# A bidirectional encoder block on one core: output projection begun where the input projection ends, modulation sums tied to tiles

## Chip, cores and metric

One core of a Trainium2 chip. The metric is the device time of one execution, in microseconds; lower is better.

## The reference

One layer on 1024 tokens of width 1024, in float32. A conditioning vector gives six modulation vectors; the input is normalised and modulated, projected once to the q, k, v of two kinds of attention, both are run, and one output projection with a gate is added to the residual. A gated feed-forward part (SwiGLU, width 2816) follows.

```python
mod = silu(c) @ w_ada + b_ada                  # six vectors: shift, scale, gate, twice
h = rms_norm(x, g_mix) * (1.0 + sc_m) + sh_m
proj = h @ w_in                                # 1024 x 3072: qa, ka, va, qb, kb, vb
o_a = neighbourhood_attention(qa, ka, va, rpb) # 8 heads of 64, window 8 x 16 on a 16 x 64 grid
o_b = differential_attention(qb, kb, vb, lam)  # 4 heads, two softmax maps each
o_b = rms_norm(o_b, subln_w) * (1 - lambda_init)
x = x + gt_m * (concatenate([o_a, o_b]) @ w_out)
h = rms_norm(x, g_ffn) * (1.0 + sc_f) + sh_f
gate, up = split(h @ w_gate_up)
x = x + gt_f * ((silu(gate) * up) @ w_down)
return rms_norm(x, g_final)
```

## The kernel before

Every large matmul is made of three, of high and low parts (high x high, high x low, low x high): a weight chunk or an activation tile is *split* into a high part, made by ScalarE (ACT), and a low part, the difference, made by VectorE (DVE) or GpSimd (POOL). For weights this is `split_into` (L201 ACT, L202 the low part, on POOL through most of attention).

The work of attention is a list of 64 *units* (`seq`): four pairs of heads of the neighbourhood attention (class `Na`), eight tiles of 128 queries each, then four heads of the differential attention (class `Da`), eight tiles each. A unit has these steps: `score` (PE's s or ns matmuls; DVE adds the bias and takes the minimum, L682 or L784, the min pass; ACT's exponential), `trans` (DVE scales, PE transposes at or nt, ACT copies the high part, DVE subtracts the low part: the unit's two *lows*, L705 or L814), `pv` (PE, for every second unit), and for `Da` `norm` and `finish` (ms, rda, bc: the norm of a head's output, which is stored to DRAM as `o_dram`).

Between these steps the main loop calls `fill(us)`, which takes matmuls off a queue of generators: the input projection's next q, k and v (`gen_qk`, `gen_v`), and at the end the first half of the output projection (`gen_mo`, matmul tiles mo, over the four pairs of the first kind of attention). `FILL` sets the amounts for each of the eight positions (pairs 0 to 3, heads 4 to 7). The second half of the output projection (tiles mpb and mp) follows when attention is done, then the feed-forward part (gu, dn).

Weights of the input projection come in 24 chunks of 512 KB: `load_next` splits the chunk that has come in and issues the load of the next, `next_w` takes a chunk. The modulation vectors that attention doesn't need are summed beside it by `gen_mods`: 48 loads wm of 256 KB, issued on POOL's queue (L587) into three buffers, and for each one step on DVE into `acc` (L596 the first of eight, L600 the others). The main loop takes one step to a unit (`next(mods, None)`). For the last unit of position 6, when the queue is empty, `load_late` loads the attention output (eight loads `ol`, L882), splits it (L888 ACT, L889 DVE), and loads, multiplies by the gate (L896) and splits the first chunks of w_out.

The program's order on each engine is not the order of the code: the scheduler that builds the program places each instruction by its own estimates, within the dependencies; `PE.after(a, b)` adds such a dependency without a semaphore, so that a stands behind b. Each engine then takes its instructions in that order.

## Time and profile before

| | us |
|---|---|
| runs (3) | 1422.79, 1429.08, 1430.99 |
| median | 1429.08 |
| the profiled execution, its own time | 1423.15 |
| its span, from the first to the last instruction | 1421.4 |

The profile holds one execution. An engine's busy time counts its own instructions; issuing a DMA or waiting for a semaphore is not busy. Matmuls are pipelined and their ends are modelled, so they overlap in the timeline. The granted clock is the share of TensorE's full clock in a stretch. The chain of waits is followed back from the last instruction, at each step to what released it. Times in the timeline count from the start of the span.

### The profile page before, as it was taken

The page shows a single profiled execution, that of the slowest core. Times are in us where ns is not written, and L with a number is a line of the kernel's source. Part 1 is how long each engine was busy: PE and PEld are TensorE (multiplying, and loading weights), DVE is VectorE, ACT ScalarE, POOL GpSimd, SP SyncE. Part 2 cuts the span into 40 slices and gives each one's busy share as a digit, 9 for nine tenths or more (in the row PEclk, how much of TensorE's full clock was granted, in tenths as well). Part 3 has the DMA queues.
Part 4 walks back from the last instruction along what each step waited for, and adds up shares of the span by engine and source line. Part 5 has one row for each costly group of instructions (what it writes and reads, how often), then busy time and mean ns, then how long its engine had stood idle before and what let it go on. Part 6 is the DMA issues. An engine that isn't in the chain of part 4 may idle for free.

```text
span 1421.4 us, 17696 instructions
## 1 busy us (share of the span) xinstructions
PE 1378.5 (97%) x7033; PEld 1142.2 (80%) x7033; DVE 724.2 (51%) x1324; ACT 461.9 (32%) x817; POOL 291.5 (21%) x318
## 2 busy tenths in 40 slices
PE   5899998999999999999999999999999999999997
PEld 5698787887898777787888888888888888888886
DVE  5775766748777589656747215113411421151136
ACT  5544444545445365423531220221121012202212
POOL 3021322311112000001430320421221132204201
PEclk8999999999999998999999999999999999999999
DMA  9231514433021251023321210211111121102102
GB/s 371 105 119 49 189 61 129 134 101 114 24 89 60 82 199 53 8 68 112 119 76 43 75 59 1 89 45 45 31 73 45 31 62 57 55 6 89 45 22 96
DMA packets 43826, 114.82 MB, mean 81 GB/s; under 512 B 12723, under 2 KB 12979, under 8 KB 42464
## 3 DMA queue, kind: packets, MB, share of 16 engines
q1 hardware_dynamic: 39280, 99.37, 20.8%
q0 software_dynamic: 4464, 14.33, 3.1%
q8 instruction: 55, 0.90, 0.3%
q14 instruction: 27, 0.22, 0.0%
HBM read 99.26 MB, written 14.42 MB: 80 GB/s over the span
## 4 chain that ended last, share of the span: by engine, by line
PE 90%; DVE 4%; ACT 2%; DMA 1%; issue 1%; POOL 1%; POOLq 0%; DVEq 0%; ACTq 0%
PE gu L89 33%; PE dn L89 17%; PE s L89 5%; PE pv L89 3%; PE mo L89 3%; PE k L89 3%; PE q L89 3%; PE mp L89 3%; PE at L89 2%; PE nk L89 2%; PE npv L89 2%; PE v1p L89 2%; PE v2p L89 2%; PE nq L89 1%; PE v3p L89 1%
## 5 line engine op out<-in xcount | busy, mean ns | idle before, releaser
L1126 DVE TENSOR_TENSOR sg<-sg,gu 128x512 f32<-128x512 f32 x44 | 30.2, 687 | 352.0 <-ACT sg L1125 352.0
L89 PE MATMUL dn<-wd_h,al 128*128 128x512 f32 x352 | 136.9, 389 | 0.0
L89 PE MATMUL dn<-wd_l,ah 128*128 128x512 f32 x352 | 136.9, 389 | 0.0
L89 PE MATMUL dn<-wd_h,ah 128*128 128x512 f32 x352 | 136.9, 389 | 0.0
L1156 DVE TENSOR_TENSOR dt<-dn,gate_f 128x512 f32<-128x512 f32 x96 | 66.4, 691 | 88.1 <-PE dn L89 88.1
L202 POOL TENSOR_TENSOR wg_l<-wg_r,wg_h 128x1024 fp32r<-128x1024 f32 x20 | 48.4, 2420 | 271.9 <-ACT wg_h L201 271.9
L684 ACT ACTIVATE p<-p,st 128x1024 f32<-128x1024 f32 x64 | 73.5, 1148 | 61.7 <-DVE st L682 58.7
L201 ACT ACTIVATE wg_h<-wg_r 128x1024 fp32r<-128x1024 f32 x22 | 23.3, 1060 | 212.2 <-PE dn L89 154.2
L89 PE MATMUL s<-qk 64*128 64x512 f32 x384 | 88.6, 425 | 2.9 <-DVE st L682 2.9
L682 DVE CUSTOM_DVE_ANT_0 p<-s,dist 128x1024 f32<-128x1024 f32 x64 | 77.1, 1218 | 23.7 <-PE s L89 22.8
L202 POOL TENSOR_TENSOR wd_l<-wd_r,wd_h 128x1024 fp32r<-128x1024 f32 x20 | 48.0, 2400 | 163.7 <-ACT wd_h L201 163.7
L89 PEld LDWEIGHTS dn<-wd_h,ah 128*128 128x128 f32 x352 | 66.1, 188 | 13.8
L89 PEld LDWEIGHTS dn<-wd_h,al 128*128 128x128 f32 x352 | 66.1, 188 | 13.7
L89 PEld LDWEIGHTS dn<-wd_l,ah 128*128 128x128 f32 x352 | 66.1, 188 | 13.7
L89 PEld LDWEIGHTS s<-qk 64*128 64x128 f32 x384 | 54.3, 189 | 26.0 <-issue 9.0
L1157 DVE TENSOR_TENSOR x<-x,dt 128x512 f32<-128x512 f32 x96 | 70.0, 729 | 2.9
L1125 ACT ACTIVATE sg<-gu 128x512 f32<-128x512 f32 x44 | 26.0, 590 | 138.4 <-PE gu L89 136.6
L89 PE MATMUL gu<-h2h,wg_h 128*128 128x512 f32 x176 | 68.9, 392 | 0.4 <-DVE sg L1126 0.4
L89 PE MATMUL gu<-h2l,wg_h 128*128 128x512 f32 x176 | 68.7, 391 | 0.0
L89 PE MATMUL gu<-h2h,wu_h 128*128 128x512 f32 x176 | 68.6, 390 | 0.0
L89 PE MATMUL gu<-h2l,wu_h 128*128 128x512 f32 x176 | 68.6, 390 | 0.0
L89 PE MATMUL gu<-h2h,wg_l 128*128 128x512 f32 x176 | 68.5, 389 | 0.0
(308 smaller groups left out, 3467.3 us busy)
## 6 DMA issues: line engine op xcount, KB each, us to landing
w_r<-in_w_in_dram SPq DMA_DIRECT2D x24, 512.0 KB, 3.7
wm<-in_w_ada_l_dram POOLq DMA_DIRECT2D x48, 256.0 KB, 3.5
wg_r<-in_w_gate_up_dram SPq DMA_DIRECT2D x22, 512.0 KB, 3.6
wu_r<-in_w_gate_up_dram SPq DMA_DIRECT2D x22, 512.0 KB, 3.5
wd_r<-in_w_down_dram SPq DMA_DIRECT2D x22, 512.0 KB, 3.5
x<-in_x_dram SPq DMA_DIRECT2D x16, 512.0 KB, 8.5
wada<-in_w_ada_s_dram SPq DMA_DIRECT2D x6, 1024.0 KB, 11.8
v<-vd SPq DMA_DIRECT2D x4, 1024.0 KB, 5.7
```

The costliest lines, as they stand in the source:

```text
L89: ins = call(*args, **kw)
L201: A.activation(out=hi, in_=raw, func=AF.Copy)
L202: lo_engine().tensor_tensor(out=lo, in0=raw, in1=hi.bitcast(F32), op=ALU.subtract)
L682: V.tensor_tensor_reduce(out=pr, in0=s, in1=dists[0][:, d0:d0 + 1024], scale=1.0, scalar=BIG, op0=ALU.add, op1=ALU.min, accum_out=self.st[ ...
L684: A.activation(out=pr, in_=pr, func=AF.Exp, scale=-1.0, bias=self.st[:, m:m + 1], accum_out=self.st[:, 2 + m:3 + m])
L1125: A.activation(out=sg, in_=gu[:, 0:512], func=AF.Silu)
L1126: V.tensor_tensor(out=sg, in0=sg, in1=gu[:, 512:1024], op=ALU.mult)
L1156: V.tensor_tensor(out=dt_, in0=out, in1=gtf[:, dsl], op=ALU.mult)
L1157: V.tensor_tensor(out=x1[i][:, dsl], in0=x1[i][:, dsl], in1=dt_, op=ALU.add)
```

## The change

Four things. (1) In `gen_qk` and `gen_v`, `load_next` stands behind the first half of a q or k, or the second of four tiles of a v, and no longer at the start. (2) `gen_mods` takes a function `mark`, and each of its steps on DVE is placed behind the instruction that `mark` names: in attention the last low that has been issued (`late_t["low"]`), in the feed-forward part the last addition of the output projection. Before, only the first step of each eight in the feed-forward part was tied. (3) `load_late` is called in the first unit of position 6 that finds the queue empty, behind that unit's `trans`; the first chunks of w_out are loaded and gated, and one is split, as soon as the last chunk of w_in has been taken (`pre_late`); o is loaded and split in two halves of four, and the second half and the chunks for the second 512 columns follow step by step, one to a unit (`late_steps`). (4) The fill of the last head is 29 for 36.

```diff
@@ -474,7 +474,6 @@
 
     def gen_qk(kind, key, name):
         w_h, w_l = next_w()
-        load_next()
         hd = key[1] + (4 if key[0][0] == "n" else 0)
         slot = qk_t(hd, 0 if kind == "q" else 2)
         mark = G.memset(slot[:, 0:1].bitcast(F32), 0.0)
@@ -491,11 +490,12 @@
                         mark = None
                 yield 0.65
             made = evac_q(out, hd, hf) if kind == "q" else evac_k(out, hd, hf)
+            if hf == 0:
+                load_next()
         qkv[key] = made
 
     def gen_v(n, evac):
         ws = [next_w(), next_w()]
-        load_next()
         for ip in range(4):
             out = bank(f"v{n}p{ip}")
             for ii in range(2):
@@ -511,6 +511,8 @@
                     if k % 2:
                         yield 0.65
             evac(n, ip, out)
+            if ip == 1:
+                load_next()
         qkv["vd", n] = True
 
     def v_tiles(n):
@@ -575,7 +577,9 @@
             tb.append(tbh)
         qkv["tb", pr] = tb
 
-    def gen_mods(steps, raw_of, acc_of, tmp_of, gate, queue, first=None, ahead=2):
+    late_t = {}
+
+    def gen_mods(steps, raw_of, acc_of, tmp_of, gate, queue, mark, ahead=2):
 
         steps = [(which, n, j) for which in steps for n in range(2) for j in range(KT)]
         raws = []
@@ -593,11 +597,11 @@
             yield
             if j == 0:
                 acc = acc_of(f"acc{which}{n}")
-                head = V.tensor_scalar(out=acc, in0=raws[at], scalar1=silc[:, 0:1], scalar2=None, op0=ALU.mult)
-                if first is not None:
-                    PE.after(head, first)
+                step = V.tensor_scalar(out=acc, in0=raws[at], scalar1=silc[:, 0:1], scalar2=None, op0=ALU.mult)
             else:
-                V.scalar_tensor_tensor(out=acc, in0=raws[at], scalar=silc[:, j:j + 1], in1=acc, op0=ALU.mult, op1=ALU.add)
+                step = V.scalar_tensor_tensor(out=acc, in0=raws[at], scalar=silc[:, j:j + 1], in1=acc, op0=ALU.mult, op1=ALU.add)
+            if mark() is not None:
+                PE.after(step, mark())
             if j < KT - 1:
                 continue
             if which in (3, 4):
@@ -702,7 +706,7 @@
                 src = tps.rearrange("p (a b) -> p a b", a=4)
                 hi, lo = at_h[b][:, :, e * P:(e + 1) * P], at_l[b][:, :, e * P:(e + 1) * P]
                 A.activation(out=hi, in_=src, func=AF.Copy)
-                V.tensor_tensor(out=lo, in0=src, in1=hi.bitcast(F32), op=ALU.subtract)
+                late_t["low"] = V.tensor_tensor(out=lo, in0=src, in1=hi.bitcast(F32), op=ALU.subtract)
 
         def pv(self, ats, pvs):
             h, i = self.h, self.i
@@ -811,7 +815,7 @@
                 src = tps[:, m * 512:m * 512 + nk].rearrange("p (a b) -> p a b", b=P)
                 dsl = (slice(None), slice(sl, sl + nk // P), slice(e * P, (e + 1) * P))
                 A.activation(out=pt_h[m][dsl], in_=src, func=AF.Copy)
-                V.tensor_tensor(out=pt_l[m][dsl], in0=src, in1=pt_h[m][dsl].bitcast(F32), op=ALU.subtract)
+                late_t["low"] = V.tensor_tensor(out=pt_l[m][dsl], in0=src, in1=pt_h[m][dsl].bitcast(F32), op=ALU.subtract)
 
         def pv(self, ats, pvs):
             pr, i = self.pr, self.i
@@ -870,9 +874,9 @@
         return gates[2]
 
     mods = gen_mods((2, 3, 4), mraw_t, lambda nm: mp.tile([P, 512], F32, tag="acc", bufs=1, name=nm),
-                    lambda nm, dt=F32: mp.tile([P, 512], dt, tag="sq", bufs=4, name=nm), gate_m, G)
-
-    oh, ol, wo, x1, late_t = [], [], [[], []], [], {}
+                    lambda nm, dt=F32: mp.tile([P, 512], dt, tag="sq", bufs=4, name=nm), gate_m, G, lambda: late_t.get("low"))
+
+    oh, ol, wo, x1 = [], [], [[], []], []
 
     o_at = {}
 
@@ -881,8 +885,8 @@
         for b in bs:
             SY.dma_start(out=o_at[n, b][1].bitcast(F32), in_=o_dram[n][:, b * 512:(b + 1) * 512])
 
-    def split_o(n, last=None):
-        for b in range(2):
+    def split_o(n, last=None, bs=(0, 1)):
+        for b in bs:
             dh, dl = o_at[n, b]
             full = last if b and last is not None else dl.bitcast(F32)
             A.activation(out=dh, in_=full, func=AF.Copy)
@@ -896,28 +900,57 @@
         V.tensor_tensor(out=both, in0=both, in1=gate, op=ALU.mult)
         wo[dh].append(split(raw, f"wo{dh}_{n2}"))
 
-    def load_late():
+    def gated(raw, dh):
+
+        both = raw.rearrange("p (a n) -> p a n", a=2)
+        gate = late_t["gtm"][:, dh * 512:(dh + 1) * 512].unsqueeze(1).to_broadcast([P, 2, 512])
+        V.tensor_tensor(out=both, in0=both, in1=gate, op=ALU.mult)
+        return raw
+
+    def pre_late():
+
         lo_eng[:] = [V]
         late_t["gtm"] = gates[2]
+        late_t["wo"] = [raw_t(f"wo0_{n2}r") for n2 in range(2)]
+        for n2, raw in enumerate(late_t["wo"]):
+            SY.dma_start(out=raw, in_=t["w_out"][0, n2])
+        for raw in late_t["wo"]:
+            gated(raw, 0)
+        wo[0].append(split_w(late_t["wo"][0], gp, "wo0_0"))
+
+    def load_late():
+
         for b in range(2):
             hi, lo = (gp.tile([P, 4, 512], F32R, tag="t8", bufs=8, name=f"o{z}{b}") for z in "hl")
             for n in range(4):
                 o_at[n, b] = hi[:, n, :], lo[:, n, :]
         for n in range(4):
-            load_o(n)
+            load_o(n, (0,))
         for n in range(4):
-            split_o(n)
-            if n % 2:
-                load_wo(0, n // 2, lambda raw, nm: split_w(raw, gp, nm))
-        ext = late_t["ext"] = qp_.tile([P, 4, S], F32R, tag="qk", name="ext")
-
-        def split(n2):
-            def f(raw, nm):
-                return split_into(raw, ext[:, 2 * n2, :], ext[:, 2 * n2 + 1, :])
-            return f
-
+            split_o(n, bs=(0,))
+            if n == 1:
+                wo[0].append(split_w(late_t["wo"][1], gp, "wo0_1"))
+        late_t["wo"] = []
         for n2 in range(2):
-            load_wo(1, n2, split(n2))
+            late_t["wo"].append(raw_t(f"wo1_{n2}r"))
+            SY.dma_start(out=late_t["wo"][-1], in_=t["w_out"][1, n2])
+            for n in (2 * n2, 2 * n2 + 1):
+                load_o(n, (1,))
+        late_t["steps"] = 0
+
+    def late_steps(upto):
+
+        while late_t["steps"] < upto:
+            i = late_t["steps"]
+            late_t["steps"] += 1
+            if i < 2:
+                for n in (2 * i, 2 * i + 1):
+                    split_o(n, bs=(1,))
+                continue
+            if i == 2:
+                late_t["ext"] = qp_.tile([P, 4, S], F32R, tag="qk", name="ext")
+            hi, lo = late_t["ext"][:, 2 * i - 4, :], late_t["ext"][:, 2 * i - 3, :]
+            wo[1].append(split_into(gated(late_t["wo"][i - 2], 1), hi, lo))
 
     def mo_part(out, dh, i, ns):
 
@@ -937,6 +970,7 @@
     def gen_mo(dh):
         dsl = slice(dh * 512, (dh + 1) * 512)
         for i in range(NT):
+            late_steps(4 if dh else 2 if i > 3 else 0)
             if dh == 0 and i % 2 == 0:
                 pair = gp.tile([P, 2, D], F32, tag="t8", bufs=8, name=f"x1_{i}")
                 for e in range(2):
@@ -946,7 +980,7 @@
             yield from mo_part(out, dh, i, range(4))
             V.tensor_tensor(out=x1[i][:, dsl], in0=out, in1=x1[i][:, dsl], op=ALU.add)
 
-    FILL = [34.0, 42.0, 24.0, 32.0, 23.0, 39.0, 34.0, 36.0]
+    FILL = [34.0, 42.0, 24.0, 32.0, 23.0, 39.0, 34.0, 29.0]
 
     SHARE = [(0.2, 0.3, 0.5), (0.25, 0.25, 0.5)]
 
@@ -981,6 +1015,8 @@
             for dh in range(2):
                 load_wo(dh, 2, lambda raw, nm: split_w(raw, gp, nm))
                 split_o(4 + dh)
+        if "steps" in late_t:
+            late_steps(min(late_t["steps"] + 1, 2 if u.pos < 7 else 4))
         share = SHARE[u.pos // 4]
         fill(step * share[0])
         if n >= 1:
@@ -993,14 +1029,16 @@
             seq[n - 3].finish()
         fill(step * share[1])
         next(mods, None)
-        if u.pos == 6 and u.i == 7:
+        if used[0] == len(PLAN) and "wo" not in late_t:
+            pre_late()
+        u.trans(ats)
+        if late_score:
+            nx.score()
+        if u.pos == 6 and "steps" not in late_t and (u.i == 7 or not queue):
             while queue:
                 fill(9)
             load_late()
             enqueue(7)
-        u.trans(ats)
-        if late_score:
-            nx.score()
         fill(step * share[2])
     for _ in mods:
         pass
@@ -1130,7 +1168,7 @@
             gtf = gate_t("gate_f")
             for _ in gen_mods((5,), lambda nm: lp.tile([P, 512], F32, tag="dt", bufs=4, name=nm),
                               lambda nm: lp.tile([P, 512], F32, tag="macc", bufs=1, name=nm),
-                              lambda nm, dt=F32: lp.tile([P, 512], dt, tag="sil", bufs=3, name=nm), lambda: gtf, SY, late_t["done"]):
+                              lambda nm, dt=F32: lp.tile([P, 512], dt, tag="sil", bufs=3, name=nm), lambda: gtf, SY, lambda: late_t["done"]):
                 pass
         wd = []
         for f in fs:
```

The order on DVE at the start of pair 1 (np, ptl: the unit's scaled exponentials and lows; acc: the modulation sums; vsl: a tile of v). Before:

```order
L803 TENSOR_SCALAR np_1_1465<-np_1_1465,nst_1_1464 128x384 x2
L814 TENSOR_TENSOR ptl_0_0_1541<-nt_0_1550,pth_0_0_1539 128x2x128
L600 SCALAR_TENSOR_TENSOR acc_1632<-wm_1410,silc,acc_1632 128x512
L814 TENSOR_TENSOR ptl_0_1_1542<-nt_0_1550,pth_0_1_1540 128x2x128
L616 TENSOR_TENSOR gate_m<-gt_1532,gb_1530 128x512
L600 SCALAR_TENSOR_TENSOR acc_1632<-wm_1537,silc,acc_1632 128x512
L600 SCALAR_TENSOR_TENSOR acc_1632<-wm_1634,silc,acc_1632 128x512
L784 ISA np_2_1591,nst_2_1590<-ns_2_1589,tb_1424 128x384
L784 ISA nst_2_1590 128x1
L784 ISA np_2_1591,nst_2_1590<-ns_2_1589,tb_1428 128x384
L784 ISA nst_2_1590 128x1
L600 SCALAR_TENSOR_TENSOR acc_1632<-wm_1709,silc,acc_1632 128x512
```

And now, from the same lows on:

```order
L818 TENSOR_TENSOR ptl_0_0_1541<-nt_0_1550,pth_0_0_1539 128x2x128
L818 TENSOR_TENSOR ptl_0_1_1542<-nt_0_1550,pth_0_1_1540 128x2x128
L600 TENSOR_SCALAR acc_1630<-wm_1340,silc 128x512
L620 TENSOR_TENSOR gate_m<-gt_1532,gb_1530 128x512
L788 ISA np_2_1591,nst_2_1590<-ns_2_1589,tb_1424 128x384
L788 ISA nst_2_1590 128x1
L788 ISA np_2_1591,nst_2_1590<-ns_2_1589,tb_1428 128x384
L788 ISA nst_2_1590 128x1
L788 ISA np_3_1662,nst_3_1661<-ns_3_1660,tb_1424 128x384
L788 ISA nst_3_1661 128x1
L540 TENSOR_TENSOR vsl_3_1609<-v3p_1512,vsh_3_1608 128x512
L788 ISA np_3_1662,nst_3_1661<-ns_3_1660,tb_1428 128x384
```

Of the four steps into acc that stood here one is left, behind the two lows of unit 0; the next stands further down, behind the lows of unit 1.

The order on PE where the output projection begins; in both, the last k matmul stands beside the transposes of unit 3 of position 6 (at_3) and the scores of its unit 5. Before (s_1: scores of unit 1 of the last head; at_7: transposes of the last unit of position 6):

```order
L89 MATMUL s_1_1_5414<-qk_4703 128x512 x6
L89 MATMUL at_7_0_5382<-ident,p_7_0_5244 128x128 x4
L89 MATMUL at_7_1_5389<-ident,p_7_0_5244 128x128 x4
L89 MATMUL mo_0_5399<-wo_0_h,oh_5326 128x512
L89 MATMUL mo_0_5399<-wo_0_h,ol_5327 128x512
```

And now (s_6: scores of unit 6 of position 6):

```order
L89 MATMUL mo_0_5217<-wo_1_h,oh_5186 128x512
L89 MATMUL mo_0_5217<-wo_1_h,ol_5187 128x512
L89 MATMUL mo_0_5217<-wo_1_l,oh_5186 128x512
L89 MATMUL s_6_1_5232<-qk_4353 128x512 x6
L89 MATMUL mo_1_5256<-wo_0_h,oh_5186 128x512
```

The first of the mo tiles has moved from behind the last unit of position 6 to ahead of the second half of the scores of its unit 6.

The order on PE at the end of attention, behind the last unit's transposes (at_7) and between its pv and its norm (ms). Before:

```order
L89 MATMUL at_7_0_6067<-ident,p_7_0_5940 128x128 x4
L89 MATMUL at_7_1_6074<-ident,p_7_0_5940 128x128 x4
L89 MATMUL mo_6_6082<-ext,oh_5328 128x512
L89 MATMUL mo_6_6082<-ext,ol_5329 128x512
L89 MATMUL mo_6_6082<-ext,oh_5328 128x512 x2
```

```order
L89 MATMUL mo_7_6124<-ext,oh_5328 128x512 x2
L89 MATMUL mo_7_6124<-ext,ol_5329 128x512
L89 MATMUL mo_7_6124<-ext,oh_5328 128x512
L89 MATMUL ms_1_6164<-mean_e,sq_1_6116 128x1 x4
L89 MATMUL bc_1_6179<-ident,rda_1_6169 128x128 x4
```

And now:

```order
L89 MATMUL mo_7_6079<-ext,oh_5188 128x512
L89 MATMUL at_7_0_6096<-ident,p_7_0_5982 128x128 x4
L89 MATMUL at_7_1_6103<-ident,p_7_0_5982 128x128 x4
L89 MATMUL pv_1_6018<-ath_3_0_6057,v_0_4828 128x256
L89 MATMUL pv_1_6018<-atl_3_0_6059,v_0_4828 128x256
```

```order
L89 MATMUL pv_1_6018<-ath_3_1_6058,v_0_4828 128x256
L89 MATMUL pv_1_6018<-atl_3_1_6060,v_0_4828 128x256
L89 MATMUL pv_1_6018<-ath_3_1_6058,v_1_4829 128x256
L89 MATMUL ms_1_6164<-mean_e,sq_1_6134 128x1 x4
L89 MATMUL bc_1_6179<-ident,rda_1_6169 128x128 x4
```

Twelve mo matmuls between at_7 and pv, and ten between pv and ms, have moved ahead of at_7; pv now follows the transposes and ms follows pv.

## Rows read from the trace of the kernel before

**Rows 1.** The page, parts 1 and 2: PE's busy time; its granted clock in 40 slices.

```profile
PE 1378.5 (97%) x7033; PEld 1142.2 (80%) x7033; DVE 724.2 (51%) x1324; ACT 461.9 (32%) x817; POOL 291.5 (21%) x318
...
PEclk8999999999999998999999999999999999999999
```

**Rows 2.** Windows: length, busy us of PE, PEld, DVE, ACT, POOL, clock, DMA, GB/s.

```profile
140.00:165.00 25.00, 22.68 (x160) 19.94 (x160) 22.42 (x51) 12.31 (x30) 8.48 (x13) 0.93 0.40 142
165.00:200.00 35.00, 35.00 (x190) 28.35 (x190) 22.35 (x60) 15.32 (x38) 10.01 (x23) 1.00 0.44 133
200.00:225.00 25.00, 20.11 (x114) 16.34 (x113) 20.05 (x46) 10.62 (x29) 7.84 (x18) 0.94 0.50 153
225.00:260.00 35.00, 34.48 (x241) 30.09 (x241) 21.65 (x63) 16.88 (x43) 7.41 (x24) 0.95 0.17 56
260.00:285.00 25.00, 23.57 (x177) 20.62 (x176) 20.55 (x55) 13.12 (x34) 11.65 (x24) 1.00 0.56 181
...
315.00:360.00 45.00, 42.45 (x195) 31.69 (x194) 33.54 (x63) 18.48 (x33) 8.78 (x10) 0.92 0.29 100
...
520.00:555.00 35.00, 34.51 (x165) 27.04 (x165) 33.83 (x61) 22.56 (x38) 1.01 (x1) 0.80 0.53 200
...
640.00:665.00 25.00, 23.40 (x104) 19.39 (x104) 15.52 (x23) 8.82 (x13) 1.09 (x2) 0.93 0.42 137
...
780.00:1421.00 641.00, 632.30 (x2790) 523.24 (x2788) 186.82 (x258) 115.19 (x165) 139.92 (x71) 1.00 0.16 51
```

**Rows 3.** The source line L600, the sums: ns min/median/max, first and last start.

```profile
L600 DVE SCALAR_TENSOR_TENSOR acc<-wm,silc,acc x56: 731/750/2964, 74.7 to 750.5; 128x512 f32<-128x512 f32 x56
```

**Rows 4.** The chain of waits from 155 to 281: start, us, what.

```profile
155.73 2.63 DVE acc L600
...
209.74 0.77 DVE acc L600
...
278.27 1.94 DVE acc L600
```

**Rows 5.** Timeline, sums on DVE and weight splits on POOL: start, us, instruction.

```profile
160.00 2.92 DVE L600 SCALAR_TENSOR_TENSOR acc<-wm,silc,acc 128x512 f32<-128x512 f32 x1
209.66 2.96 DVE L600 SCALAR_TENSOR_TENSOR acc<-wm,silc,acc 128x512 f32<-128x512 f32 x1
...
155.41 2.38 POOL L202 TENSOR_TENSOR w_l<-w_r,w_h 128x1024 fp32r<-128x1024 f32 x1 [0.78 <-ACT w_h L201]
159.98 2.39 POOL L202 TENSOR_TENSOR w_l<-w_r,w_h 128x1024 fp32r<-128x1024 f32 x1
209.67 2.40 POOL L202 TENSOR_TENSOR w_l<-w_r,w_h 128x1024 fp32r<-128x1024 f32 x1
277.26 2.39 POOL L202 TENSOR_TENSOR w_l<-w_r,w_h 128x1024 fp32r<-128x1024 f32 x1
```

**Rows 6.** Windows, the weight splits on POOL alone: length, busy us, clock, DMA.

```profile
140.00:345.00 205.00, 25.50 (x11) 0.97 0.38 124
```

**Rows 7.** Timeline of PE, SP and DVE where the output projection begins.

```profile
519.65 0.40 PE L89 MATMUL k<-hh,w_l 128*128 128x512 f32 x1
...
550.91 0.48 PE L89 MATMUL mo<-wo_h,oh 128*128 128x512 f32 x1
...
514.87 3.64 SPq L882 DMA_DIRECT2D ol<-o_dram  x8
...
527.61 1.89 DVE L889 TENSOR_TENSOR ol<-ol,oh 128x512 fp32r<-128x512 f32 x3
```

**Rows 8.** Timeline of PE, DVE and ACT at the end of attention.

```profile
633.92 0.48 PE L89 MATMUL mo<-ext,oh 128*128 128x512 f32 x1
...
634.40 0.69 DVE L705 TENSOR_TENSOR atl<-at,ath 128x512 fp32r<-128x512 f32 x1 [2.42 <-ACT ath L704]
...
640.26 0.60 ACT L725 ACTIVATE sq<-pv 128x512 f32<-128x512 f32 x1 [5.40 <-PE pv L89]
...
644.90 0.79 PE L89 MATMUL bc<-ident,rda 128*128 128x128 f32 x4 [1.60 <-DVE rda L745]
```

## The prediction

> **What bounds the kernel now.** I read the page first. TensorE (PE) is busy 97% of the span, and its granted clock is full but for a few slices of the first half [rows 1]: PE's own work sets the time, and all that a reordering can win is time in which PE stands idle or runs at the lower of its two levels (1.2 against 2.4 GHz). Then the windows view, by stage [rows 2]. Behind 780 us, in the feed-forward part, PE is busy 632.30 of 641 us at clock 1.00, and the change moves nothing there; so the question is the attention part. For each stretch I count idle time (length minus PE busy) plus clock loss (one minus the granted clock, times the length). 165 to 200: nothing, and DVE is busy 22.35 of 35 us, 64%. 140 to 165: 2.32 + 1.75 = 4.1 us. 200 to 225: 4.89 + 1.50 = 6.4. 225 to 260: 0.52 + 1.75 = 2.3. 260 to 285: 1.43 + 0 = 1.4. 315 to 360: 2.55 + 3.60 = 6.2. 520 to 555: 0.49 + 7.00 = 7.5. 640 to 665: 1.60 + 1.75 = 3.4. Together 31 us, and no reordering of this kind can give more than that. In the stretches that lose, DVE is the late engine: 22.42 of 25 us busy in the first, 33.83 of 35 in the sixth.
>
> Then what DVE does there. A modulation sum takes 0.75 us [rows 3]; attention has 48 of them, in six bursts of eight, and the four stretches from 140 to 285 that lose hold three bursts. In these, single sums last far longer: 2.63 us from 155.73, 2.92 from 160.00, 2.96 from 209.66, 1.94 from 278.27, and the chain of waits runs through three of them [rows 4, 5]. Each of the four stands beside a weight split on POOL (2.38 to 2.40 us), and each ends 0.55 to 0.57 us after that split has ended (155.41 + 2.38 = 157.79 against 158.36, and so on). Over 0.75 us each, the four hold DVE 1.88 + 2.17 + 2.21 + 1.19 = 7.5 us. 11 such splits run from 140 to 345 us, 25.5 us of 205 [rows 6].
>
> Last the seam at 520. The last k matmul starts at 519.65, the first mo matmul at 550.91 [rows 7]. For 31 us PE has only scores, transposes and pv, whose pace DVE sets, and DVE also carries all eight o splits, the last three from 527.61 to 529.50.
>
> **The change, part by part.** *Sums tied.* Nothing is added: 48 sums of 0.75 us, 36 us of DVE, are done either way. The order shows one sum behind the lows of each unit, where a burst of eight stood beside the first units of a pair. That lifts some five sums of 0.75 us and the holds off each burst and puts them into stretches where DVE is 64% busy. A wm load is issued when the sum three places ahead has read its buffer; one sum to a unit leaves it two units (some 13 us: the bursts, a pair's eight units apart, come 54 us after each other) to land, so a sum waits for no load. Three bursts lose 4.1 + 6.4 + 2.3 + 1.4 = 14.2 us. Bounds: 0, if the start of a pair (tables, first scores, q and k evacuations) costs this anyway, and 14.2. I take two thirds, **9 us**, because the chain goes through the sums themselves in all three but in the second also through other work of DVE and ACT. The fourth burst, eight sums (5.7 us) in 315 to 360, stands beside the change from one kind of attention to the other: of 6.2 us I take a third, **2 us** (bounds 0 and 6.2).
>
> *Weight loads and splits tied to a half or a tile (load_next).* The order has every split of w_in on POOL behind the same PE work as before, and its first use as far away; SP's loads swap places by a few rows. 0 us. The sums of the feed-forward gate don't move in the order either: 0.
>
> *Output projection begun early.* 192 mo matmuls stay 192. The first now stands one unit's scores, 24 pv and eight transposes behind the last k matmul. What it needs: the four o loads of the first half, which wait for the buffers that k frees and go out from 514.87, some 5 us before k ends [rows 7], then four splits on ACT and DVE and the split of wo0_1, all of which now stand ahead of that unit's min passes on DVE. I work out some 1 us of PE idle there (four ol of 0.6, the wo split 1.2, q/k evacuation 0.6 and one ol of 0.6, then the min pass 1.2: the scores of the next unit, which need its PSUM buffer, can start about 6 us after k, and PE comes there after 5). From then on mo fills PE while DVE works off the same splits, later and spread. Of 7.5 us I take **5** (bounds 0, if the o splits are late by as much, and 7.5).
>
> *The end of attention.* Fewer mo matmuls are left for the end: the order has no mo between the last transposes and the last pv, and none between pv and ms, where twelve and ten stood. That cover goes. The last low of the first half is ready at 634.40 + 0.69 = 635.1, while PE stood ready at 633.9: 1.1 us. The squares that ms needs take 640.26 to 640.86, so about 0.7 us more. The wait for bc (1.60) stays [rows 8]. 1.8 us of idle, and a second drop of the clock like the one now there (1.75) or none: +1.8 to +3.6, I take **+2.5**. Nothing else of the change adds a wait.
>
> Sum: -9 - 2 - 5 + 2.5 = -13.5 us. Against the profiled execution's 1423.15 us that is 1409.6. That execution stands at the lower end of the three runs (1422.79 to 1430.99, median 1429.08); a median of the changed kernel may stand anywhere in the like spread, so I add some 2 us: **1412 us**.
>
> **A rule against it.** The row first: the long sums end with the split on POOL, not with a load [rows 4, 5]. The Trainium skill, "SBUF — State Buffer", section "Who interferes with whom", says that a DVE instruction with two inputs in SBUF and a GpSimd instruction that reads SBUF exclude each other for a whole instruction. The trace agrees, with the 0.55 us above. By that rule tying the sums to units removes no split and frees no port; by it alone the result is the second rival below, near 1417 us.
>
> **The rivals.** (1) *All is regained*: each burst's loss goes and the seam closes: -14.2 - 4 - 7.5 + 1.8 = -24, 1399 us. For it: quiet stretches between the bursts lose nothing. Against it: pairs must still start.
>
> (2) *The sums are caught by the splits again.* The splits fill 25.5 / 205 = 12% of the time [rows 6], so of 30 scattered sums some 3.7 are caught, for half a split (1.2 us): 4.5 us, where four now lose 7.5. Then the bursts give only 3, the switch of attention 1: -3 - 1 - 5 + 2.5 = -6.5, 1417 us: no difference that shows. Against it: the order puts most splits on POOL right behind a wm load that waits for a sum, so the next sum is a unit away.
>
> (3) *Slower.* Each sum now stands behind the unit's last lows and ahead of a min pass, in the chain from one unit to the next; in the bursts of before it stood where DVE was late anyway. If the pairs' starts cost what they cost without the sums (gain 0), and sums and holds land on the path, each costs 0.75. From (5 - 2.5 + 7) / 0.75 = 13 of the 48 on, the kernel is slower by over 7 us; with 20 (15 us) it is -5 + 2.5 + 15 = +12.5, 1436 us. Against it: DVE's 64% between bursts.
>
> (4) *The early mo blocks.* PE takes its work in order, so if o's splits are late, mo holds the scores behind it. Then the seam gives 0 and the rest stays: -9 - 2 + 2.5 = -8.5, 1415 us, just faster.
>
> **How the numbers follow.** 0.5% is 7 us, about what a measurement of this kernel can tell from no change. My forecast has 0.5, rival 1 0.15, rival 2 0.18, rival 3 0.07, rival 4 0.10. Faster: 0.5 + 0.15 + most of rival 4, and the lower edge of rival 2 against the higher median: 0.76. Same: 0.17. Slower: 0.07. The range goes from rival 1, 1399, to rival 2 at the higher end of the runs' spread (1417 + 6 = 1423): 1399 to 1423.
>
> **What would show it.** Right: no sum on DVE of over 1.5 us in the attention part, or one or two; PE idle below 1 us and clock 1.00 at the starts of pairs 1 to 3; first mo matmul within 10 us of the last k; the 35 us behind k at clock 0.9 or better; three idle places at the end of attention, some 3.4 us together. Wrong: idle at the pairs' starts as large as now with the sums gone from there (pairs, not sums, cost it); small idle times all over the first attention (rival 3); new drops of the clock at the end of attention that eat more than the 2.5 us; or a changed time behind 780 us.

## The result and the profile after

The changed kernel took 1409.55 us (median of four runs, 1402.55 to 1410.91), the kernel before beside it 1428.37: a ratio of 0.9866, 95% interval [0.9837, 0.9894], some 19 us less. A second series (run 11 below) gave 1407.38 us (1406.09 to 1409.40) beside 1427.41, ratio 0.9861 [0.9839, 0.9884]. The forecast was 1412 us, 1399 to 1423, faster with a chance of 0.76.

The profiled executions differ by 13.8 us (1423.15 and 1409.35). That of before is one of the shorter of its runs, that of after is at its median, so the rest of the 19 us is in the choice of the profiled run. First the page of after, parts 1 and 2: busy time by engine and the granted clock.

```profile
PE 1370.6 (97%) x7033; PEld 1136.7 (81%) x7033; DVE 719.6 (51%) x1324; ACT 461.0 (33%) x817; POOL 290.3 (21%) x318
...
PEclk7999999999999999999999999999999999999999
```

Against [rows 1]: the same 7033 matmul records, but PE is busy for 7.9 us less (1378.5 - 1370.6), and of the 13.8 us of span only 5.9 are idle time of PE. More than half of the gain is thus time that the same matmuls no longer spent at 1.2 in place of 2.4 GHz; the clock columns of the windows say the same (17.4 us of clock loss from 140 to 665 us before [rows 2], 6.6 after; of the difference the first 140 us take some 2 back). DVE does the same work (724.2 and 719.6 us).

Then the windows of after, the same stretches and columns as [rows 2].

```profile
140.00:165.00 25.00, 25.00 (x181) 22.29 (x180) 19.52 (x55) 13.29 (x33) 8.09 (x12) 1.00 0.48 172
165.00:200.00 35.00, 35.00 (x194) 28.52 (x193) 21.86 (x55) 14.31 (x35) 10.66 (x25) 1.00 0.42 124
200.00:225.00 25.00, 23.60 (x141) 19.11 (x140) 17.98 (x49) 12.97 (x33) 7.23 (x22) 1.00 0.42 117
225.00:260.00 35.00, 34.28 (x274) 31.20 (x274) 29.60 (x79) 17.96 (x48) 9.94 (x30) 1.00 0.34 118
260.00:285.00 25.00, 25.00 (x168) 21.59 (x168) 17.48 (x47) 13.51 (x33) 9.49 (x20) 1.00 0.49 168
...
315.00:360.00 45.00, 44.62 (x238) 34.30 (x236) 36.30 (x72) 23.05 (x41) 5.90 (x7) 1.00 0.13 42
360.00:520.00 160.00, 156.12 (x942) 126.66 (x941) 114.41 (x209) 75.33 (x127) 21.33 (x21) 0.97 0.29 103
520.00:555.00 35.00, 35.00 (x187) 27.40 (x186) 31.42 (x60) 16.12 (x27) 1.01 (x1) 1.00 0.19 68
```

From 140 to 285 us, 14.2 us of idle time and clock loss have become 1.40 + 0.72 = 2.1, and the clock is 1.00 in every one of these rows. 165 to 200, quiet before, stayed quiet. 315 to 360: 6.2 us has become 0.4. 520 to 555: 7.5 has become 0, but the seam is earlier now. And 360 to 520, which lost nothing before (a clock of 1.00 and 160.00 us busy), now loses 3.88 us of idle time and has a clock of 0.97. First its row in the kernel before; then, in the changed kernel, the windows of two places inside it and of the end of attention:

```profile
360.00:520.00 160.00, 160.00 (x1000) 131.31 (x998) 115.57 (x217) 76.53 (x129) 20.72 (x18) 1.00 0.20 69
```

```profile
425.00:450.00 25.00, 22.69 (x111) 17.66 (x110) 19.54 (x35) 11.62 (x20) 4.68 (x6) 0.86 0.12 43
505.00:520.00 15.00, 13.43 (x71) 10.17 (x70) 13.48 (x21) 11.38 (x20) 0.00 (x0) 0.89 0.97 358
605.00:640.00 35.00, 32.03 (x174) 26.70 (x173) 20.23 (x35) 11.88 (x20) 1.14 (x2) 0.95 0.39 130
```

505 to 520 is what is left of the seam: 1.57 + 1.65 = 3.2 us. 425 to 450 is new: 2.31 + 3.5 = 5.8 us. The timeline of DVE, POOL and PE there (start, us, instruction):

```profile
437.67 2.25 DVE L602 SCALAR_TENSOR_TENSOR acc<-wm,silc,acc 128x512 f32<-128x512 f32 x1
439.84 1.21 DVE L686 CUSTOM_DVE_ANT_0 p<-s,dist 128x1024 f32<-128x1024 f32 x1
440.99 0.68 DVE L461 SCALAR_TENSOR_TENSOR qk<-q,qk 128x512 fp32r<-128x512 f32 x1
...
436.91 2.46 POOL L202 TENSOR_TENSOR w_l<-w_r,w_h 128x1024 fp32r<-128x1024 f32 x1 [6.72 <-ACT w_h L201]
...
441.72 0.79 PE L89 MATMUL k<-hh,w_h 128*128 128x512 f32 x1 [2.31 <-DVE qk L461]
```

One of the tied sums met a split: 2.25 us in place of 0.74, ending 0.55 us after the split, the sign of [rows 5]. The min pass and the evacuation of q stand behind it on DVE, k needs the buffer that this evacuation frees, and PE waits 2.31 us; then its clock is at the lower level. Of the 48 sums of the attention part two last over 1.5 us, this one and one at 228.14 (2.57 us), behind which PE didn't wait; before there were four [rows 4, 5]. The row that answers to [rows 3], the sums:

```profile
L602 DVE SCALAR_TENSOR_TENSOR acc<-wm,silc,acc x56: 736/744/2566, 99.4 to 736.0; 128x512 f32<-128x512 f32 x56
```

### The profile page after: what moved, and what is told of

It reads as the page before. It is cut to its first block, busy times and chain, and to the rows that moved or that the text cites. A ratio compares the mean times of both kernels' runs of the same rounds, so it can differ in the third digit from the quotient of the medians.

```text
span 1407.6 us, 17672 instructions
## 1 busy us (share of the span) xinstructions
PE 1370.6 (97%) x7033; PEld 1136.7 (81%) x7033; DVE 719.6 (51%) x1324; ACT 461.0 (33%) x817; POOL 290.3 (21%) x318
## 4 chain that ended last, share of the span: by engine, by line
PE 91%; DVE 3%; ACT 2%; DMA 2%; issue 1%; POOL 1%; SPq 0%; DVEq 0%; POOLq 0%; ACTq 0%
PE gu L89 33%; PE dn L89 17%; PE s L89 5%; PE pv L89 3%; PE mo L89 3%; PE q L89 3%; PE k L89 3%; PE nk L89 2%; PE mp L89 2%; PE npv L89 2%; PE at L89 2%; PE v1p L89 2%; PE v0p L89 2%; PE v3p L89 2%; PE v2p L89 2%; PE nq L89 2%
## 5 line engine op out<-in xcount | busy, mean ns | idle before, releaser
L89 PE MATMUL s<-qk 64*128 64x512 f32 x384 | 82.5, 415 | 1.5 <-DVE st L686 1.5
L89 PEld LDWEIGHTS dn<-wd_h,al 128*128 128x128 f32 x352 | 66.1, 188 | 13.7
L89 PEld LDWEIGHTS dn<-wd_h,ah 128*128 128x128 f32 x352 | 66.1, 188 | 13.7
L89 PEld LDWEIGHTS dn<-wd_l,ah 128*128 128x128 f32 x352 | 66.1, 188 | 13.7
L89 PEld LDWEIGHTS s<-qk 64*128 64x128 f32 x384 | 50.9, 184 | 22.7 <-issue 8.1
L591 POOL DMA_DIRECT2D wm<-in_w_ada_l_dram x48 | 27.4, 570 | 202.2 <-DVE acc L602 100.7
## 6 DMA issues: line engine op xcount, KB each, us to landing
wada<-in_w_ada_s_dram SPq DMA_DIRECT2D x6, 1024.0 KB, 12.1
```

The source lines that it names most:

```text
L89: ins = call(*args, **kw)
L591: queue.dma_start(out=raws[-1], in_=t["w_ada_l"][which - 2, n, :, j, :])
```

## The experiments

Medians stand beside those of the kernel before on the same chip.

**1. The sums alone.** The kernel before with the changed `gen_mods` (code cut; the low parts of both kinds of attention are kept in `late_t`):

```
+            if mark() is not None:
+                PE.after(step, mark())
...
-                V.tensor_tensor(out=lo, in0=src, ...)
+                late_t["low"] = V.tensor_tensor(out=lo, in0=src, ...)
```

> The kernel before with the sums alone tied to the low parts of o and of the probabilities; weight loads and output projection as before. Theory (bursts of sums, and the POOL splits that hold them, make DVE late at the starts of the pairs): the losses of 140 to 285 us and of 315 to 360 go, the seam at 520 stays: 9 to 17 us less than the kernel before, and at most some four sums over 1.5 us. Rival (a pair's start costs this anyway, sums or not): within 3 us of the kernel before. Rival (the scattered sums are caught by the splits again): 3 to 6 us less, with as many sums over 1.5 us as before.

Measured: 1410.0 us (1408.83 to 1413.44) against 1426.48, ratio 0.9886 [0.9867, 0.9906]: 16.5 us less, two sums over 1.5 us. Its windows: the three stretches of the bursts in one, the fourth burst, and the seam:

```profile
140.00:285.00 145.00, 142.88 (x950) 122.74 (x949) 106.36 (x282) 71.85 (x181) 45.39 (x106) 1.00 0.45 137
315.00:360.00 45.00, 44.62 (x237) 34.35 (x237) 36.33 (x71) 22.91 (x41) 5.78 (x7) 1.00 0.13 42
505.00:545.00 40.00, 34.15 (x181) 26.00 (x180) 37.60 (x69) 25.32 (x42) 1.01 (x1) 0.91 0.51 186
```

The first row is that of the changed kernel to a few hundredths (142.88 busy there too). The third shows the seam, untouched and no better than before: 5.85 + 3.6 = 9.5 us lost in 40, where the kernel before lost 7.5 [rows 2]. So nearly the whole gain is the sums', and both rivals fall: pairs' starts don't cost it, and the splits don't take it back, but for the one at 437, which stands in this kernel too (2.26 us at 437.78).

**2. The output projection alone.** The changed kernel with the sums in bursts (`lambda: None` as the mark) and `load_next()` back at the start of a projection.

> The changed kernel with its sums in bursts again and its weight loads where they were: the early output projection alone. Theory (the seam gives 3 to 5 us, the end of attention takes 1 to 2.5 back): 1 to 4 us less than the kernel before, PE idle at the starts of the pairs as before. Rival (the output projection is the larger part of the gain): 8 us less or more. Rival (it moves the loss only, the end takes back what the seam gave): within 1 us.

Measured: 1423.16 us (1418.01 to 1426.70) against 1426.48, ratio 0.9978 [0.9964, 0.9992]: 3.3 us less.

```profile
505.00:545.00 40.00, 40.00 (x221) 31.20 (x219) 35.01 (x64) 22.47 (x40) 1.75 (x2) 1.00 0.52 191
635.00:660.00 25.00, 22.03 (x105) 18.31 (x104) 9.05 (x14) 7.48 (x11) 1.01 (x1) 0.86 0.34 116
```

The seam is closed altogether, 0 us lost; the end of attention loses 2.97 + 3.5 = 6.5 us, where the kernel before lost 3.4 [rows 2]. Closed 7.5, given back 3.1: by these rows 4.4 us, by the runs 3.3. The two parts add up: 16.5 + 3.3 = 19.8, and the whole change gives 19 to 20.

**3. The weight loads and splits alone.**

```
-        load_next()
...
+            if hf == 0:
+                load_next()
```

> The kernel before with the weight loads and splits alone tied to the first half or tile of a projection. Theory (the splits keep their place behind the same work of PE): within 2 us of the kernel before. Rival (splits that begin a few us later or earlier meet other work on DVE, and this is part of the gain): 3 us or more away, with the splits of 150 to 285 us beginning at least 2 us away from where they stood against PE's work.

Measured: 1427.66 us against 1426.48, ratio 1.0002 [0.9990, 1.0015]. This part is worth nothing, as the theory had it.

**4. Without the sums, in the kernel before.** `else:` ahead of the step at L600 becomes `elif queue is SY:`, which leaves out seven of the eight steps of each sum of the attention part; their loads stay.

> The kernel before; seven of the eight steps of each modulation sum of the attention part are left out (42 of its 48 operations on DVE), their loads stay. What bursts and holds together cost, by taking them away. Theory (they make DVE late at the pairs' starts): 12 to 20 us less than the kernel before, PE idle below 1 us at the starts of pairs 1 to 3. Rival (the pairs' starts cost it anyway): within 4 us of the kernel before.

Measured: 1410.32 us against 1426.48, ratio 0.9888 [0.9864, 0.9911].

```profile
140.00:285.00 145.00, 140.20 (x934) 120.34 (x933) 93.66 (x262) 71.88 (x180) 44.92 (x102) 1.00 0.44 139
```

and two of the waits of PE in this stretch (us, times, longest):

```profile
PE q L89 <- POOL w_l L202: 1.5, 1, 1.5
PE nq L89 <- POOL w_l L202: 0.8, 1, 0.8
```

16.2 us less, the number of run 1. Taking 42 sums away gives no more than tying them: tied, they cost nothing that shows. In part the rival is right: 4.80 us of PE idle time stay, most of it in five places of 0.53 to 1.47 us, and two of these are over the 1 us that the theory allowed. But 2.3 us of it are these two waits, of nq and q for a weight split on POOL, which the kernel before doesn't have in this stretch. The other 2.5 us, waits for DVE and ACT, are what the starts cost by themselves here, a sixth of the 15 us that the stretch lost before; the clock stays at 1.00.

**5. Without the sums, in the changed kernel.** The same edit at L602.

> The changed kernel; seven of the eight steps of each modulation sum of the attention part are left out (42 of its 48 operations on DVE), their loads stay. What the tied sums still cost. Theory (tied, they stand where DVE has room, and only the sum held at 437 us costs anything): 3 to 7 us less than the changed kernel, all of it in 360 to 520 us. Rival (tied sums stand in the chain from unit to unit, 0.75 us each): over 10 us less, spread over the attention part.

Measured: 1406.44 us against 1426.43, ratio 0.9855 [0.9836, 0.9875], 1 to 3 us below the two medians of the changed kernel. PE is busy 160.00 of 160 us from 360 to 520, so the loss at 437 is gone; waits of nq and q for weight splits on POOL, 1.39 and 1.65 us at 161.7 and 275.5, came in its stead. The theory's 3 to 7 us is met beside the first of the two medians only. The rival (sums on the chain from unit to unit) asked for over 10 us and falls.

**6. Splits in four pieces, in the kernel before.** Are the sums' places or their holds the price?

```
-        lo_engine().tensor_tensor(out=lo, in0=raw, ...)
+        e = lo_engine()
+        for q in range(4 if e is G else 1):
+            c = slice(256 * q, 256 * q + 256) if e is G else slice(0, 1024)
+            e.tensor_tensor(out=lo[:, c], in0=raw[:, c], ...)
```

> The kernel before with the low part of each weight split on POOL made in four operations of 128 x 256 in place of one of 128 x 1024. A sum that is held by a split waits for one piece, 0.6 us, and not for 2.4. Theory 1 (the holds are what the bursts cost): no sum over 1.5 us, and 5 to 9 us less than the kernel before. Theory 2 (five displaced sums of 0.75 us in a burst are what it costs, and the holds lie beside other waits): the long sums go, but under 3 us of time.

Measured: 1418.76 us (1416.13 to 1420.69) against 1426.43, ratio 0.9942 [0.9921, 0.9963]. The two holds of the first burst are gone; two sums are still held, in the second and third burst, and so one kernel shows bursts with a hold beside one without. The windows of the three:

```profile
140.00:165.00 25.00, 25.00 (x184) 22.36 (x183) 20.69 (x52) 13.28 (x33) 11.24 (x20) 1.00 0.42 140
...
200.00:225.00 25.00, 20.16 (x106) 16.12 (x106) 20.70 (x45) 10.85 (x28) 8.95 (x22) 0.87 0.51 148
...
260.00:285.00 25.00, 24.59 (x173) 21.00 (x171) 21.27 (x54) 13.92 (x36) 12.19 (x28) 1.00 0.51 160
```

and the timeline of sums and pieces:

```profile
159.00 0.97 DVE L603 SCALAR_TENSOR_TENSOR acc<-wm,silc,acc 128x512 f32<-128x512 f32 x1
...
206.61 3.39 DVE L603 SCALAR_TENSOR_TENSOR acc<-wm,silc,acc 128x512 f32<-128x512 f32 x1
...
274.43 2.37 DVE L603 SCALAR_TENSOR_TENSOR acc<-wm,silc,acc 128x512 f32<-128x512 f32 x1 [0.44 <-DMA wm<-in_w_ada_l_dram]
...
156.34 4.23 POOL L205 TENSOR_TENSOR w_l<-w_r,w_h 128x256 fp32r<-128x256 f32 x4 [0.26 <-ACT w_h L201]
...
206.61 2.83 POOL L205 TENSOR_TENSOR w_l<-w_r,w_h 128x256 fp32r<-128x256 f32 x4
```

All three stretches hold a burst of eight sums at the start of a pair. In the first, 0.97 us is the longest, and PE loses nothing; in the second, one sum is held for 3.39 us and 4.84 + 3.25 = 8.1 us are lost; in the third, the last sum is held for 2.37 us and PE loses 0.41. In the kernel before, the first burst with its two holds lost 4.1 us, the second 6.4 and the third 1.4 [rows 2]. So DVE can bear the first burst without its holds, and a hold of over 2 us costs much in one place and next to nothing in another. That is theory 1 for the first burst alone, and not as it was put: the same sums of the second and third burst are held as before, for longer (2.96 and 1.94 us before). At 206.61 the four pieces follow one another without a gap, and the sum ends 0.56 us after the last of them (206.61 + 2.83 = 209.44, against 210.00).

**7. The same pieces in the changed kernel.**

> The changed kernel with the same four pieces. Theory (the sum held at 437 us for 2.25 us, and the drop of PE's clock behind it, cost some 5 us): no sum over 1.5 us, clock 1.00 at 441 us, 3 to 7 us less than the changed kernel. Rival (PE would have lost it there in another way): within 2 us of the changed kernel, a drop of the clock elsewhere between 360 and 520 us.

Measured: 1408.94 us against 1426.43, ratio 0.9872 [0.9852, 0.9892], the changed kernel's own number. The sum at 440 took 1.32 us, k waited 1.39 and the clock stayed up there, but another sum was held for 2.93 us at 273.73, mo waited 1.14 at 540.7, and the clock was lower for longer at the end of attention. Nothing is won: the rival.

**8. More output projection for the end.** The last entry of `FILL`, 29.0, becomes 26.0.

> The changed kernel with less output projection put between the last units of attention (26 in place of 29 in the last entry of the table of fillers), so that more mo matmuls are left to stand between the last transposes, the last pv and ms. Theory (the cover that the early start took from the end cost 1 to 2 us of idle time there): the idle places ahead of pv and ms (0.3 and 0.7 us) go, 1 to 2 us less than the changed kernel, or up to 4 if the clock doesn't fall. Rival (the last units then lack filler): as much idle time comes back before 620 us, time the same or 1 to 3 us more.

Measured: 1405.6 us (1403.43 to 1409.96) against 1426.43, ratio 0.9855 [0.9831, 0.9878]. The three idle places at the end are as long as before to a hundredth (0.34, 0.69, 1.69): the mo that the table gave back went ahead of the last transposes. The theory's cause didn't happen, and the ratios don't tell the two kernels apart. The profile, 4.9 us shorter, shows by what executions with the same waits differ:

```profile
425.00:450.00 25.00, 22.69 (x124) 18.10 (x123) 19.54 (x37) 11.63 (x20) 4.68 (x6) 0.93 0.13 43
505.00:520.00 15.00, 13.47 (x75) 9.82 (x74) 13.46 (x24) 11.68 (x20) 0.00 (x0) 1.00 0.99 379
```

Beside the same two rows of the changed kernel, above, the idle time is the same to 0.04 us, and the clock is 0.93 for 0.86 and 1.00 for 0.89: the same waits, and 1.75 + 1.65 = 3.4 us less of low clock behind them.

**9. The end of attention tied.** Run 8 raised the question why filler stands ahead of transposes whose input is ready. In `trans`, `pv` and `norm` the last PE instruction is kept in `late_t["tr"]`, `["pv"]`, `["ms"]`; `PE.hold = a` places the next instruction on PE behind a:

```
+    seq[-1].norm(units)
     for i in range(2):
         for dh in range(2):
+            PE.hold = (None, late_t["tr"], late_t["pv"], late_t["ms"])[2 * i + dh]
             run(mo_part(outs[i][:, dh * 512:(dh + 1) * 512], dh, i, (4, 5)))
-    seq[-1].norm(units)
```

> The changed kernel with three of the four blocks of six mpb matmuls tied behind the last transposes, the last pv and ms. In the changed kernel the last probabilities are ready on DVE at 613.75 us, but their transposes stand behind 24 mpb and 12 mo matmuls, at 622.84; then PE waits 0.25 + 0.34 + 0.69 + 1.69 us. Theory (the order, not the engines, makes the end of attention wait): these idle places together fall below 1 us, the clock stays at 1.00 there, 2 to 5 us less than the changed kernel. Rival (DVE or ACT is late there): the wait stands ahead of the last transposes, time within 1 us.

Measured: 1405.26 us (1403.84 to 1409.20) against 1427.41, ratio 0.9850 [0.9822, 0.9877]; the changed kernel beside it 1407.38. PE of the changed kernel first, with its four waits, then of this one:

```profile
624.13 0.38 PE L89 MATMUL pv<-ath,v 128*128 128x256 f32 x1 [0.25 <-ACT ath L708]
624.85 0.39 PE L89 MATMUL pv<-atl,v 128*128 128x256 f32 x1 [0.34 <-DVE atl L709]
628.56 1.05 PE L89 MATMUL ms<-mean_e,sq 128*128 128x1 f32 x8 [0.69 <-ACT sq L729]
631.30 0.62 PE L89 MATMUL bc<-ident,rda 128*128 128x128 f32 x4 [1.69 <-DVE rda L749]
```

```profile
615.87 0.50 PE L89 MATMUL mo<-ext,oh 128*128 128x512 f32 x1 [0.47 <-DVE x L981]
625.24 0.95 PE L89 MATMUL ms<-mean_e,sq 128*128 128x1 f32 x8
627.87 0.62 PE L89 MATMUL bc<-ident,rda 128*128 128x128 f32 x4 [0.18 <-DVE rda L749]
```

2.97 us of waits have become 0.18, 0.47 us came earlier, and the clock stays at 1.00. In the profiles that is 4.6 us (1409.40 and 1404.78), in the medians 2.1. The place was one of order, as the theory had it; the size in the runs is too near their spread to be settled.

**10. And the held sum a unit later.** In `gen_mods`, behind the `yield` of a step; the sum at 437, step 44 of 48, and the three behind it come a unit later:

```
+            if queue is G and at == 44:
+                yield
```

> The kernel of the run with the tied end, and the sum that a split holds at 437 us (step 44 of 48) made one unit later, behind the next low part. Theory (that hold costs 2.3 us of idle time and up to 3.4 us of clock): no wait of k at 441 us, 2 to 6 us less than the kernel with the tied end alone. Rival (the later sums are caught by another split, or the wait comes back in another form): within 1.5 us, with another long sum or another idle place over 1 us between 425 and 480.

Measured: 1403.12 us (1399.81 to 1404.01) against 1427.41, ratio 0.9825 [0.9802, 0.9848]. Its windows at the place of the wait, and at the seam:

```profile
425.00:450.00 25.00, 24.86 (x148) 20.35 (x147) 20.59 (x40) 11.99 (x21) 4.96 (x6) 1.00 0.24 73
500.00:520.00 20.00, 17.20 (x76) 13.06 (x75) 18.30 (x32) 12.64 (x23) 0.00 (x0) 0.78 0.90 337
```

The wait of k and the drop of the clock are gone, and one sum over 1.5 us is left. Some of it came back 70 us later, at the seam, which now loses 2.80 + 4.4 = 7.2 us (3.4 in the changed kernel by the same window): pv waited 1.71 us there in place of 0.30, and the clock was low for longer. Theory and rival are both half right: beside run 9 the medians differ by 2.1 us, and the runs of the two overlap. All five runs of this kernel are shorter than the shortest of the changed kernel beside it (1404.01 against 1406.09): by the medians it is 4.3 us shorter than the changed kernel and 24 us shorter than the one before.

**11. The changed kernel again.**

> The changed kernel itself, beside the two before on the same chip: 1403 to 1411 us. What its runs differ by, and where.

Measured: 1407.38 us (1406.09 to 1409.40), given above. The profile of this execution has the wait at 441.8 (2.32 us), the low clock behind it and the waits at the end of attention again. The time of 1402.55 us in the first series, at a granted clock of 0.991 against 0.984 or 0.985 in the other three, was not met again; which of these drops it was spared was not recorded.

## Why the prediction was right, point by point

**The bursts (9 us) and the fourth (2 us).** Right in cause for the first three, low in size. By the windows, 14.2 - 2.1 = 12.1 and 6.2 - 0.4 = 5.8 us: 17.9 us where the sum had 11. The step that was mis-sized is "I take two thirds" and "a third": nearly all of it was the sums', also where the chain went through other work of DVE and ACT. Runs 1, 4 and 6 say so: these starts of pairs lose 2.1 us together with the sums tied (run 1), 4.8 without them (run 4; 2.5 but for the waits for weight splits), and the first alone nothing with its burst and without its holds (run 6); no clock is lost in any of the three. The rival that the pairs cost it had 0 to 14.2 as its bounds; it is worth some 2 to 2.5 of them. In the fourth burst no sum was over 1.5 us before, and tying gave the most of it all the same (run 1: 0.4 us lost there, as in after); 3.6 of the 6.2 us were clock. How much of it is the burst's isn't settled: with its eight sums in place the stretch lost 1.6 us in run 6 and 13.7 in run 2, of which 0 and 12.2 are clock, and with them tied or left out 0.4 in every run.

**Sums against splits.** The forecast's sum had no term for a tied sum that meets a split; the second rival had, at 4.5 us spread over 3.7 sums. Two sums of 48 were caught, and of them one cost 5.8 us and the other nothing. So this rival was right that it happens and wrong that it makes the result: what a hold costs depends on whether PE is waiting behind it (in run 6 holds of 3.39 and 2.37 us stood in bursts that lost 8.1 and 0.4 us), and the mean of 1.2 us hides this. Less this, the term for the sums is 17.9 - 5.8 = 12.1 us, near the 11 of the forecast by two errors that cancel.

The rule of the Trainium skill ("SBUF — State Buffer", section "Who interferes with whom") that the prediction names agrees with every run that has such a case: a sum that begins while an uncut split runs ends 0.55 to 0.57 us after it. What the rule doesn't give is the price; that is in the rows of PE.

**load_next (0 us).** Right: run 3.

**The seam (5 us).** 7.5 - 3.2 = 4.3 us by the windows, in run 2 the whole 7.5, and beside run 1, whose seam lost 9.5, it is 6.3; over the 40 us from 505 the clock is 0.89 for 15 us and then 1.00, as was said. The first mo matmul stands at 518.70, the last k at 506.89: 11.8 us and not 10. PE's idle places there are 0.30 and 0.18 us for pv and 1.08 for the scores, which wait for a min pass behind o splits and the wo split; the forecast had "some 1 us" by the same queue. It left out the clock: 1.65 us behind these waits.

**The end of attention (+2.5 us).** In after 2.97 us of idle time and a clock of 0.95 (1.75), 4.7 us where 3.4 stood [rows 2]: +1.3 us in after, +3.1 in run 2. The three places were those named (the first, ahead of pv, in two parts); they sum to 2.97 us, against 3.4 in the forecast. That it was the price of an early start was right, that it must be paid wasn't: run 9 takes the idle time away by order alone.

**The sum.** -12.1 - 5.8 + 5.8 - 4.3 + 1.3 = -15.1 us, against 13.8 between the profiles; the first 140 us, which this sum leaves out, take some 0.5 us (1.3 less of idle time, 1.8 more of clock), and the rest is rounding, of the clock to hundredths above all. The working gave 1409.6 us, and the profiled run took 1409.35. That it came so near is luck: the term of the sums was 7 us too small and that of the caught sum, put at nothing, 6 us, and the two cancel. The 2 us that were added for the runs' spread were not there: the profiled run of before lies 3 to 5 us under the medians of 1426 to 1428, that of after at its median, so the medians differ by 19.

**The signs.** Two long sums (one or two were asked for); clock 1.00 at the pairs' starts, but one idle place of 1.40 us at 216.4 where below 1 us was asked for; first mo 11.8 us behind k and not 10; nothing changed behind 780 us but that it begins earlier. A new drop of the clock was named as a sign of error for the end of attention; it came at 441.

**Slower** (rival 3) was excluded by runs 1 and 5: the tied sums brought nearly the whole gain, and taking them away gave 1 to 3 us more, not over 10. **Rival 4** (late o splits, so that the seam gives nothing) falls with the seam's 4.3 us. **Rival 1** (all is regained, 1399 us) is what the kernel of run 10 comes near to, with 1403.

## What to carry to other kernels

Where an engine that feeds the bottleneck has a burst of work that nobody waits for, tie it piece by piece to the steps of the main loop: here this gave as much as leaving the work out (runs 1 and 4). Then look where a piece stands beside an operation that blocks its engine, and move that one alone: of two held sums, the one in front of an evacuation cost 5.8 us at its place and the other nothing; measure the whole then, since moving it cost some 4 us at the seam (run 10). And before filler is said to be missing at the end of a stage, look whether it stands ahead of work whose input had long been ready.

## What the runs showed of the hardware

A split of 128 x 1024 on POOL held not only sums: a TENSOR_TENSOR on DVE of 128 x 1 (L744, both inputs in SBUF) took 2.25 us in place of 0.15, and a TENSOR_SCALAR of np (L807, one tensor in SBUF and a scalar to each partition) 2.08 in place of 0.41. Operations of DVE beside the same splits that read their tensor from PSUM kept their time: the low part of at, 0.68 us at 437.07, and an evacuation of q, 0.69 at 324.82, beside the split of 324.44. Cutting a split into four pieces released DVE in some places (0.97 us at 159.00) and not in others (3.39 at 206.61, where the pieces followed each other without a gap); and four pieces took 2.83 us where one operation took 2.40.

The clock was the larger half of the gain between the two profiles, and it is also what runs of one kernel differ by: of the runs of before beside run 1, the shortest took 1422.33 us at a granted clock of 0.980 and the longest 1430.85 at 0.972. The same wait of k, 2.31 us, was followed by a clock of 0.86 over its 25 us in one execution and 0.93 in another (run 8); a wait of 1.40 us (nt, at 216 to 218) by 1.00 over 200 to 225 us in the changed kernel and by 0.93 in the kernel of run 10. And the clock fell without any wait: in run 2, whose profiled execution was the longest of its runs, the windows around 322 us are

```profile
315.00:322.00 7.00, 7.00 (x30) 4.89 (x29) 1.71 (x4) 1.11 (x3) 2.39 (x1) 1.00 0.23 75
322.00:340.00 18.00, 17.70 (x55) 13.27 (x55) 12.68 (x26) 7.06 (x13) 2.17 (x4) 0.53 0.38 132
```

PE was busy for all of the first, with q, then scores of 64 partitions and npv of 128 x 256, and then worked at 1.2 GHz for most of 18 us: 8.5 us lost. The kernel before did the same work there, 7.00 of 7 us busy, and kept 1.00 until it had waited 1.35 us at 329 (0.91 over 322 to 340). Why one execution falls and another doesn't is open; that fewer idle places leave fewer such falls is what the page's 7.9 us suggest, and no run here tried the clock by itself.
